# Compression blocks laid out by pairs of neighbouring positions, with one weight transfer per unit

## The chip, the cores and the metric

One core of a Trainium2 chip runs the whole two-layer decoder trunk as a single program. The metric is the device time in microseconds of one execution; the median of 3 runs before the change is 643.1 us (642.93 to 644.03).

## The reference, cut to what matters

The trunk has a gated convolution layer, a SwiGLU layer, sparse attention with three branches and a second SwiGLU layer, for 256 tokens of 1024 features, all in float32. The change touches the compressed branch of the attention alone:

```
L_CMP, D_CMP, G, DH = 32, 16, 4, 64        # block length, step, groups, head size
def compress(kv_raw, pe, w1, w2):           # once for keys, once for values
    idx = arange(15)[:, None] * D_CMP + arange(L_CMP)[None, :]
    blocks = kv_raw[:, idx] + pe            # 15 blocks of 32 tokens, overlapping by 16
    blocks = blocks -> [15, G, 32 * 64]
    return silu(blocks @ w1) @ w2           # w1: 2048 x 256, w2: 256 x 64
```

Block n covers the tokens 16n to 16n+31, so each token stands in two blocks. The position embedding pe is the same for every block; its product with w1 is added to each block's result as a share.

## The kernel before, in words

Every float32 operand of a matrix product is held as a high part (rounded by a copy on ScalarE) and a low part (the rest, a subtraction on VectorE), and a product is two or three matmuls. A weight comes in units of up to 128 x 1024. `split_weights` (L302) issues the unit's transfer on SP's queue into one of four raw buffers, copies the high part on ScalarE (L322), and subtracts on VectorE or GpSimd (L326). `Stream.ahead` issues a unit, `take` hands it to the matmuls.

The stage between the first SwiGLU layer and the attention follows a list of items, CFG["plan"]. K, Q, V and Y are projection units, Y being w1 (two sets st, four units q each); CR scales a projection into cf (L762); CB builds the blocks (`cmp_blocks`, L764); Y multiplies (`cmp_piece`, L780); J, M, t, ck, cv finish the compression. Between the marks `|4` and `|5` of the plan no engine's order is written out: a planner with a cost model of its own orders the instructions of all engines, SP's queue with them. From `|5` on TensorE follows the plan, and the planner orders the other engines. CB0 and CB1 and the first Y units stand between the two marks.

cf holds the compressed keys or values with features on the partitions: two groups above each other on 64 partitions each, two pairs of groups side by side, 256 tokens. `cmp_blocks` makes of it the stationary operand xc, 128 partitions x (high and low) x 4 groups x 256 columns: the upper 64 partitions hold token t, the lower 64 token t+16. That takes four ScalarE copies (L777) and four VectorE subtractions (L778) for each st, each of 64 partitions x 480 elements. The last 16 columns hold pe (L772, through `split`, L418 and L421), which thereby becomes a sixteenth block.

`cmp_piece` multiplies: for each of 16 positions lp in the half block, the stationary operand is the 128 columns (high and low, group, block n) that lie 16 elements apart, and the moving one 256 columns of w1's high part (L788), then of its low part (L789): 64 matmuls for both st. Since w1 lies in memory with rows of two neighbouring positions above each other, and the operand has positions lp and lp+16 above each other, each unit comes in two transfers of 64 rows (L314 to L316).

pe is loaded early, in the convolution stage, into a constant tile peT by two small transfers (L632). In that stage TensorE's and GpSimd's orders are as written (L597).

Of the kernel before, what the change touches and what calls it, by code (L numbers as in the profile page):

```python
# [10 lines left out]
AF = mybir.ActivationFunctionType  # L11
ALU = mybir.AluOpType
# [4 lines left out]
P = 128  # L17
D = 1024
S = 256
# [4 lines left out]
G = 4  # L24
DH = 64
NCMP = 16
# [201 lines left out]
def trunk(ctx: ExitStack, tc: tile.TileContext, a):  # L228
    nc = tc.nc
# [11 lines left out]
    def in_order(*engines):  # L241

        if "order" in phase:
            phase.pop("order").close()
        if engines:
            phase["order"] = ctx.enter_context(ExitStack())
            phase["order"].enter_context(tc.manual_schedule(engines=set(engines)))
# [14 lines left out]
    def bank(name, kind="short", hold=False):  # L262

        b = min((b for b in ring[kind] if b not in held.values()), key=used.get)
        touch(b)
        if hold:
            held[name] = b
        return psum.tile([P, 512], F32, tag=f"b{b}", name=name)
# [7 lines left out]
    def f(ap):  # L276
        return ap.bitcast(F32)

    def four(name):
        return [bank(f"{name}_{b}", "long") for b in range(4)]  # L280
# [4 lines left out]
    def pair(name, shape, rows=P):  # L285

        return act.tile([rows, 2, *shape], F32R, tag="pair", name=name, bufs=3)

    def one(name, cols=S, rows=P, dt=F32):

        return tmp.tile([P, S + 2], dt, tag="one", name=name, bufs=8)[:rows, :cols]
# [10 lines left out]
    def split_weights(src, name, cols, ring, pool):  # L302
        if (name[0], ring) in spare:
            w, hi, lo = spare.pop((name[0], ring))
        else:
            if phase["name"] == "attention" or name[0] == "O" or name[:2] == "kv":
                w = wp.tile([P, 1024], F32, tag="raw", name=f"w_{name}", bufs=4)
            else:
                w = phase["pool"].tile([P, 1024], F32, tag="raw", name=f"w_{name}", bufs=12)
            hi, lo = (wp.tile([P, 1024], F32R, tag=ring + hl, name=f"{hl}_{name}", bufs=3) for hl in "hl")  # L310
            if name[0] == "O":
                spare[name[0], ring] = [x[:, cols:] for x in (w, hi, lo)]
            w, hi, lo = (x[:, :cols] for x in (w, hi, lo))
        if isinstance(src, list):  # L314
            for r, part in enumerate(src):
                nc.sync.dma_start(out=w[r * DH:(r + 1) * DH], in_=part)  # L316
        else:
            nc.sync.dma_start(out=w, in_=src)
        if pool in ("hi", "all"):
            nc.gpsimd.tensor_copy(hi, w)  # L320
        else:
            nc.scalar.activation(hi, w, AF.Copy)  # L322
        cut = {False: 0, True: cols, "both": cols // 2, "hi": 0, "all": cols}[pool]
        for eng, c0, c1 in ((nc.gpsimd, 0, cut), (nc.vector, cut, cols)):
            if c0 < c1:
                eng.tensor_tensor(out=lo[:, c0:c1], in0=w[:, c0:c1], in1=f(hi[:, c0:c1]), op=ALU.subtract)  # L326
        return hi, lo
# [33 lines left out]
    takes = {}  # L361
# [4 lines left out]
            takes[f"Q{s}{'ab'[p]}"] = a["w_q"][s, p], 1024  # L366
    for q in range(4):
        for st in range(2):

            w1 = a["w1"][st, q % 2 * DH:(q % 2 + 1) * DH]  # L370
            takes[f"Y{st}{q}"] = [w1[:, x * 1024:(x + 1) * 1024] for x in (q // 2, 2 + q // 2)], 1024
        takes[f"V{q}"] = a["w_v"][q], 1024
    takes["GP"] = a["w_g"], KC * 48

# [41 lines left out]
    def split(hi, lo, src, key="ad"):  # L416
        if key[0] == "a":
            nc.scalar.activation(hi, src, AF.Copy)  # L418
        else:
            nc.gpsimd.tensor_copy(hi, src)  # L420
        (nc.gpsimd if key[1] == "p" else nc.vector).tensor_tensor(out=lo, in0=src, in1=f(hi), op=ALU.subtract)  # L421
# [8 lines left out]
    peT = const.tile([P, 2, NCMP], F32, name="peT")  # L430
# [79 lines left out]
    def residual_step(accs, u, x, first, chunks=range(KC)):  # L510
        for o in chunks:
            mm3(acc_at(accs, o), columns(u, o), x, first and o % 2 == 0, False)
# [36 lines left out]
    def stream_in(c, n=1):  # L549
        nc.sync.dma_start(out=h[:, c:c + n], in_=xT[:, c:c + n])  # L550
        for i in range(c, c + n):
            n0.high(i)
            n0.low(i)
# [10 lines left out]
    def conv_proj(pcv, pb, u, k0, n=2):  # L564
        for k in range(k0, k0 + n):
            for i, o in enumerate((pcv[:, :S], pcv[:, S:], pb[:, :S])):
                col = (3 * (k - k0) + i) * P
                mm3(o, sl(u, ALL, slice(col, col + P)), sl(x0, ALL, k), k == 0 and i != 1, k == KC - 1)
# [20 lines left out]
    def hidden(m, name):  # L589
        mh, ml = (phase["pool"].tile([P, S], F32R, tag=f"m{hl}", name=f"{name}_{hl}", bufs=4) for hl in "hl")  # L590
        split(mh, ml, m)
        return mh, ml

    ps, us, accs = {}, {}, None
    for j in range(KC):
        if j == 1:
            in_order(*ORD[9])  # L597

        ps[j] = [bank(f"{n}{j}", "long" if j == 2 else "short") for n in ("pcv", "pb")]
        for p in range(4):  # L600
            if j == 0 and p == 0:
                for k in range(2):
                    conv_proj(*ps[j], wa.take(), k, 1)
                    wa.ahead()
                    if k == 0:
                        stream_in(6, 2)
            else:
                conv_proj(*ps[j], wa.take(), 2 * p)
                wa.ahead()
            if j == 0:  # L610
                n0.square(2 * p)
                n0.square(2 * p + 1)
            if j == 1 and p == 1:
                n0.rstd()
            if j == 1 and p == 2:
                n0.spread()
                nc.vector.tensor_tensor(out=r2, in0=n0.bc, in1=n0.bc, op=ALU.mult)
                us[0] = conv_rest(0, *ps[0])
            if p == 2 and j:
                wr.ahead(min(j, 3))  # L620
            if p == 1 and j >= 2:
                gated.append(hidden(us[j - 1], f"m{j - 1}"))
            if p == 3 and j == 1:
                gated.append(hidden(us[0], "m0"))
        if j:
            us[j] = conv_rest(j, *ps[j])
        if j == 1:
            for t, n in ((dist, "dist"), (cdist, "cdist"), (rowvis, "rowvis")):
                nc.sync.dma_start(out=t, in_=a[n])
            for half in range(2):  # L630
                rows = slice(half * DH, half * DH + DH)
                nc.sync.dma_start(out=peT[rows], in_=a["peT"][rows, :, half * NCMP:(half + 1) * NCMP])  # L632
        if j == 2:
            accs = four("acc0")
        if j >= 2:
            residual_step(accs, wr.take(), gated[j - 2], j == 2)
# [121 lines left out]
    cf, xc, ys_, w2s, py = {}, {}, {}, {}, {}  # L758
# [5 lines left out]
    def cmp_blocks(st):  # L764

        if not xc:
            blocks = pair("xc", [2, G, S])
            xc.update({i: blocks[:, i] for i in range(2)})  # L770
        pe = peT[:, st].unsqueeze(1).to_broadcast([P, G, NCMP])
        split(xc[st][:, 0, :, S - 16:], xc[st][:, 1, :, S - 16:], pe)  # L772
        for gp in range(2):
            for half in range(2):
                src = cf[st][gp * DH:gp * DH + DH, :, 16 * half:S - 16 + 16 * half]
                dst = xc[st][half * DH:half * DH + DH, :, gp::2, :S - 16]
                nc.scalar.activation(dst[:, 0], src, AF.Copy)  # L777
                nc.vector.tensor_tensor(out=dst[:, 1], in0=src, in1=f(dst[:, 0]), op=ALU.subtract)  # L778

    def cmp_piece(st, q):  # L780
        if q == 0:
            py[st] = bank(f"py{st}", hold=True)
        wh, wl = wa.take()
        for i in range(4):
            lp = 8 * (q // 2) + 2 * i + q % 2
            first, last = q == 0 and i == 0, q == 3 and i == 3
            x = xc[st].rearrange("p hl g (n l) -> p l (hl g) n", l=16)[:, lp]
            nc.tensor.matmul(py[st][:, :256], x, wh[:, i * 256:(i + 1) * 256], start=first, stop=False)  # L788
            nc.tensor.matmul(py[st][:, :256], x, wl[:, i * 256:(i + 1) * 256], start=False, stop=last)  # L789

# [333 lines left out]
    for item in plan:  # L1124
        m = re.match(r"([A-Z|][A-Z]?|[a-z]+)(.*)", item)
# [40 lines left out]
    for t in range(2):  # L1166
        ms = EPS

        for c, part in ((0, slice(0, 512)), *((1, slice(x, x + n)) for n in (512 // (t + 1),)
# [5 lines left out]
            cols = slice(c * 512 + part.start, c * 512 + part.stop)  # L1175
# [3 lines left out]
            else:  # L1179
                nc.vector.tensor_tensor(out=hT[:, t, c * 512:(c + 1) * 512], in0=accs[2 * t + c],  # L1180
                                        in1=hT[:, t, c * 512:(c + 1) * 512], op=ALU.add)
# [6 lines left out]
            m = tmp.tile([P, 1], F32, tag="ms", name=f"fin_ms{t}{cols.start}", bufs=3)  # L1188
# [85 lines left out]
```

## Time and profile before

| | |
|---|---|
| median of 3 runs | 643.1 us (642.93 to 644.03) |
| profiled execution | 642.83 us, its span 641.0 us |
| granted TensorE clock, mean | 0.995 |
| TensorE busy | 619.5 us of the span, 97% |
| VectorE busy | 471.2 us, 74% |
| ScalarE busy | 377.4 us, 59% |
| GpSimd busy | 279.4 us, 44% |
| transfers | 109.53 MB, mean 171 GB/s |

The span runs from the first to the last instruction; what lies around it is 1.83 us. The convolution takes about the first 100 us, the first SwiGLU layer lasts to about 290 us, projections, compression and attention to about 440 us, and the second SwiGLU layer takes the rest. A busy engine is one with an instruction under way. TensorE's matmuls overlap in the pipeline, so the distance between starts, not the duration of one, is what a matmul costs.

### The profile page before, as it was taken

Reading aid. Unit: us, or ns where it says so; the run is one execution under the profiler, and the core shown is the slowest. Engines: PE = TensorE matmul, PEld = TensorE weight load, DVE = VectorE, ACT = ScalarE, POOL = GpSimd, SP = SyncE. Lnnn points to the kernel's source line nnn. Section 1 sums busy time; section 2 is a strip of 40 time slices with the busy share of each in tenths; the row PEclk is TensorE's granted clock in tenths of the full one; section 3 lists DMA queues with packets and bytes.
Section 4 is the critical chain, followed back from the end, with each engine's and each line's share of the span. In section 5 each row is a group of like instructions: output and inputs, shape, how many; then the busy total and the mean of one; then the engine's idle time right before and its main releaser. Section 6 shows DMA issues by size and latency. Waiting matters only on the chain.

```text
span 641.0 us, 11285 instructions
## 1 busy us (share of the span) xinstructions
PE 619.5 (97%) x4158; PEld 568.4 (89%) x4158; DVE 471.2 (74%) x783; ACT 377.4 (59%) x738; POOL 279.4 (44%) x258
## 2 busy tenths in 40 slices
PE   7999999999999999999999999997999999999995
PEld 6999999889999999999989998986888888888894
DVE  5789767866666666679996899787876666666664
ACT  7454447464455555547766988986565555555433
POOL 4054313854443334315100756567754433344423
PEclk9999999999999999999989999999999999999998
DMA  8996672646555554032978410009946655555001
GB/s 289 357 351 216 220 237 94 230 165 201 194 196 183 181 177 152 2 99 68 238 196 258 159 67 2 34 2 361 399 158 198 196 182 182 176 184 165 1 1 66
DMA packets 36360, 109.53 MB, mean 171 GB/s; under 512 B 5713, under 2 KB 8145, under 8 KB 36305
## 3 DMA queue, kind: packets, MB, share of 16 engines
q1 hardware_dynamic: 36160, 108.55, 51.2%
q8 instruction: 33, 0.54, 0.3%
q10 hardware_dynamic: 144, 0.26, 0.1%
q14 instruction: 23, 0.18, 0.1%
HBM read 107.22 MB, written 1.05 MB: 169 GB/s over the span
## 4 chain that ended last, share of the span: by engine, by line
PE 81%; DVE 10%; POOL 4%; issue 2%; DMA 1%; ACT 1%; SPq 0%; POOLq 0%; DVEq 0%; ACTq 0%
PE pgu L658 21%; PE pgu L660 11%; PE acc L397 4%; PE acc L398 4%; PE acc L396 4%; PE acc L726 3%; PE acc L725 3%; PE acc L724 3%; PE pcv L398 2%; DVE n L451 2%; PE pcv L397 2%; PE pcv L396 2%; PE po L1060 1%; POOL l_d L326 1%; PE pgu L398 1%
## 5 line engine op out<-in xcount | busy, mean ns | idle before, releaser
L658 PE MATMUL pgu<-n,h_gu 128*128 128x512 f32 x640 | 226.8, 397 | 2.9 <-DVE n L451 2.8
L660 PE MATMUL pgu<-n,l_gu 128*128 128x256 f32 x640 | 179.3, 281 | 1.1 <-DVE l_gu L326 1.1
L658 PEld LDWEIGHTS pgu<-n,h_gu 128*128 128x128 f32 x640 | 120.1, 188 | 31.0 <-DVE n L451 3.0
L326 DVE TENSOR_TENSOR l_gu<-w_gu,h_gu 128x1024 fp32r<-128x1024 f32 x88 | 117.1, 1332 | 26.6 <-ACT h_gu L322 26.1
L672 POOL TENSOR_TENSOR gu<-gu,n_rbc 128x512 f32<-128x512 f32 x40 | 54.8, 1374 | 166.1 <-DVE gu L667 150.0
L660 PEld LDWEIGHTS pgu<-n,l_gu 128*128 128x128 f32 x640 | 121.0, 189 | 2.3 <-DVE l_gu L326 1.4
L680 DVE TENSOR_TENSOR av<-sg,gu 128x256 f32<-128x256 f32 x44 | 74.4, 1692 | 65.7 <-ACT sg L678 65.5
L326 POOL TENSOR_TENSOR l_d<-w_d,h_d 128x1024 fp32r<-128x1024 f32 x40 | 98.0, 2452 | 4.9 <-ACT h_d L322 4.4
L322 ACT ACTIVATE h_gu<-w_gu 128x1024 fp32r<-128x1024 f32 x88 | 92.6, 1053 | 7.1 <-PE pb L397 3.5
L322 ACT ACTIVATE h_d<-w_d 128x1024 fp32r<-128x1024 f32 x44 | 46.8, 1063 | 27.1 <-PE acc L726 21.2
L418 ACT ACTIVATE a_h<-av 128x256 fp32r<-128x256 f32 x44 | 18.3, 416 | 72.8 <-DVE av L680 72.8
L678 ACT ACTIVATE sg<-gu 128x256 f32<-128x256 f32 x44 | 18.2, 416 | 58.9 <-POOL gu L672 54.2
L397 PE MATMUL acc<-a_l,h_d 128*128 128x256 f32 x176 | 49.5, 282 | 0.3 <-DVE a_l L421 0.3
L396 PE MATMUL acc<-a_h,h_d 128*128 128x256 f32 x176 | 49.3, 282 | 0.5 <-ACT a_h L418 0.5
L398 PE MATMUL acc<-a_h,l_d 128*128 128x256 f32 x176 | 49.3, 281 | 0.0
L326 DVE TENSOR_TENSOR l_in<-w_in,h_in 128x768 fp32r<-128x768 f32 (+1 forms) x33 | 38.8, 1187 | 11.4 <-ACT h_in L322 11.4
L322 ACT ACTIVATE h_in<-w_in 128x768 fp32r<-128x768 f32 (+1 forms) x33 | 27.1, 824 | 30.4 <-PE pb L397 21.8
L398 PE MATMUL pcv<-n,l_in 128*128 128x256 f32 x128 | 36.8, 288 | 1.8 <-DVE l_in L326 1.7
L396 PE MATMUL pcv<-n,h_in 128*128 128x256 f32 x128 | 36.8, 287 | 1.7 <-ACT h_in L322 1.7
L397 PE MATMUL pcv<-n,h_in 128*128 128x256 f32 x128 | 36.4, 284 | 0.0
L665 ACT ACTIVATE gu<-pgu 128x256 f32<-128x256 f32 x80 | 29.6, 370 | 10.9 <-PE pgu L660 10.9
L724 PE MATMUL acc<-h_d,a_h 128*128 128x512 f32 (+1 forms) x88 | 34.8, 395 | 0.0
(428 smaller groups left out, 1666.2 us busy)
## 6 DMA issues: line engine op xcount, KB each, us to landing
w_gu<-in_w_gu SPq DMA_DIRECT2D x88, 512.0 KB, 4.2
w_d<-in_w_down SPq DMA_DIRECT2D x44, 512.0 KB, 3.4
w_in<-in_w_in SPq DMA_DIRECT2D x31, 384.0 KB, 6.4
w_wo<-in_w_out SPq DMA_DIRECT2D x8, 512.0 KB, 6.3
w_kvY<-in_w SPq DMA_DIRECT2D x16, 256.0 KB, 5.1
w_kvV<-in_w_v SPq DMA_DIRECT2D x4, 512.0 KB, 5.9
h<-in_xT SPq DMA_DIRECT2D x3, 256.0 KB, 6.2
out<-y SPq DMA_DIRECT2D x3, 256.0 KB, 2.3
```

The costliest lines, as they stand in the source:

```text
L322: nc.scalar.activation(hi, w, AF.Copy)
L326: eng.tensor_tensor(out=lo[:, c0:c1], in0=w[:, c0:c1], in1=f(hi[:, c0:c1]), op=ALU.subtract)
L396: nc.tensor.matmul(out, wh, xh, start=start, stop=False, skip_group_check=True)
L397: nc.tensor.matmul(out, wh, xl, start=False, stop=False, skip_group_check=True)
L398: nc.tensor.matmul(out, wl, xh, start=False, stop=stop, skip_group_check=True)
L658: nc.tensor.matmul(ps[j][c], uh[:, cols], x[:, :, k], start=k == 0, stop=False, skip_group_check=True)
L660: nc.tensor.matmul(ps[j][c][:, :S], ul[:, cols], x[:, 0, k], start=False, stop=k == KC - 1, skip_group_check=True)
L665: nc.scalar.activation(gus[j][:, c], ps[j][c][:, S:], AF.Copy)
L672: nc.gpsimd.tensor_tensor(out=gu, in0=gu, in1=norm.bc.unsqueeze(1).to_broadcast([P, 2, S]), op=ALU.mult)
L680: nc.vector.tensor_tensor(out=av, in0=sg, in1=gu[:, 1], op=ALU.mult)
L724: nc.tensor.matmul(out, xh, wh, start=start, stop=False, skip_group_check=True)
L725: nc.tensor.matmul(out, xh, wl, start=False, stop=False, skip_group_check=True)
```

## The change

The operand xc is laid out by pairs. The upper 64 partitions hold the even tokens, the lower 64 the odd ones, so that a column j is the pair of tokens 2j and 2j+1. It is stored twice, "late" = 0 and late = 1, the second copy shifted by 16 tokens (8 pairs). Each copy has its last 8 columns for pe. The tile has as many bytes as before. A st now takes eight copies and eight subtractions of 64 partitions x 240 elements, which read cf at every second token. The columns of a stationary operand lie 8 elements apart instead of 16; the number of matmuls is the same. Rows of w1 are used as they lie, so a unit is one transfer of 128 rows; the list form of `split_weights` goes. pe is loaded by one transfer into a temporary tile of the tag "one" (8 buffers), and two GpSimd copies sort its even and odd positions into peT.

```diff
-        if isinstance(src, list):
-            for r, part in enumerate(src):
-                nc.sync.dma_start(out=w[r * DH:(r + 1) * DH], in_=part)
-        else:
-            nc.sync.dma_start(out=w, in_=src)
+        nc.sync.dma_start(out=w, in_=src)
...
-            w1 = a["w1"][st, q % 2 * DH:(q % 2 + 1) * DH]
-            takes[f"Y{st}{q}"] = [w1[:, x * 1024:(x + 1) * 1024] for x in (q // 2, 2 + q // 2)], 1024
+            takes[f"Y{st}{q}"] = a["w1"][st, :, q * 1024:(q + 1) * 1024], 1024
...
+            pe = one("pe", cols=4 * NCMP).rearrange("p (st m two) -> p st m two", st=2, two=2)
+            nc.sync.dma_start(out=pe.rearrange("p st m two -> p st (m two)"), in_=a["peT"])
             for half in range(2):
                 rows = slice(half * DH, half * DH + DH)
-                nc.sync.dma_start(out=peT[rows], in_=a["peT"][rows, :, half * NCMP:(half + 1) * NCMP])
+                nc.gpsimd.tensor_copy(peT[rows], pe[rows, :, :, half])
...
-            blocks = pair("xc", [2, G, S])
-            xc.update({i: blocks[:, i] for i in range(2)})
-        pe = peT[:, st].unsqueeze(1).to_broadcast([P, G, NCMP])
-        split(xc[st][:, 0, :, S - 16:], xc[st][:, 1, :, S - 16:], pe)
+            blocks = pair("xc", [2, 2, G, P])
+            xc.update({i: blocks[:, i].rearrange("p late hl g j -> p hl late g j") for i in range(2)})
+        pe = peT[:, st].rearrange("p (late m) -> p late m", late=2).unsqueeze(2).to_broadcast([P, 2, G, 8])
+        split(xc[st][:, 0, :, :, P - 8:], xc[st][:, 1, :, :, P - 8:], pe)
         for gp in range(2):
-            for half in range(2):
-                src = cf[st][gp * DH:gp * DH + DH, :, 16 * half:S - 16 + 16 * half]
-                dst = xc[st][half * DH:half * DH + DH, :, gp::2, :S - 16]
-                nc.scalar.activation(dst[:, 0], src, AF.Copy)
-                nc.vector.tensor_tensor(out=dst[:, 1], in0=src, in1=f(dst[:, 0]), op=ALU.subtract)
+            for odd in range(2):
+                dst = xc[st][odd * DH:odd * DH + DH, :, :, gp::2, :P - 8]
+                for late in range(2):
+                    src = cf[st][gp * DH:gp * DH + DH].rearrange("p c (j two) -> p c j two", two=2)[
+                        :, :, 8 * late:P - 8 + 8 * late, odd]
+                    hi, lo = dst[:, 0, late], dst[:, 1, late]
+                    nc.scalar.activation(hi, src, AF.Copy)
+                    nc.vector.tensor_tensor(out=lo, in0=src, in1=f(hi), op=ALU.subtract)
...
-            lp = 8 * (q // 2) + 2 * i + q % 2
+            late, m = divmod(4 * q + i, 8)
             first, last = q == 0 and i == 0, q == 3 and i == 3
-            x = xc[st].rearrange("p hl g (n l) -> p l (hl g) n", l=16)[:, lp]
+            x = xc[st][:, :, late].rearrange("p hl g (n m) -> p m hl g n", m=8)[:, m]
+            x = x.rearrange("p hl g n -> p (hl g) n")
```

## Rows read from the trace of the kernel before

**Rows 1.** The page's busy times of the engines over the whole span.

```profile
PE 619.5 (97%) x4158; PEld 568.4 (89%) x4158; DVE 471.2 (74%) x783; ACT 377.4 (59%) x738; POOL 279.4 (44%) x258
```

**Rows 2.** Windows: length, busy time of each engine, granted clock, DMA share, GB/s.

```profile
0.00:40.00 40.00, 34.75 (x255) 33.12 (x256) 27.29 (x42) 23.46 (x41) 13.17 (x20) 1.00 0.94 339
...
302.00:322.00 20.00, 19.90 (x166) 19.90 (x167) 18.50 (x29) 13.44 (x20) 3.34 (x2) 1.00 0.80 211
322.00:331.00 9.00, 7.79 (x38) 7.11 (x36) 8.87 (x12) 5.22 (x8) 0.00 (x0) 0.96 0.80 207
331.00:354.00 23.00, 23.00 (x134) 21.68 (x134) 16.97 (x27) 15.43 (x26) 1.57 (x3) 0.94 0.86 256
```

**Rows 3.** The timeline of TensorE around the first products of the blocks: start, duration.

```profile
322.21 0.28 PE L398 MATMUL pkv<-n,l_kvK4b 128*128 128x256 f32 x1
322.33 0.39 PE L788 MATMUL py<-h_kvY,xc 128*128 128x256 f32 x1
322.56 0.38 PE L789 MATMUL py<-l_kvY,xc 128*128 128x256 f32 x1
...
326.88 0.27 PE L788 MATMUL py<-h_kvY,xc 128*128 128x256 f32 x1
328.37 0.49 PE L789 MATMUL py<-l_kvY,xc 128*128 128x256 f32 x1 [1.22 <-DVE l_kvY L326]
```

**Rows 4.** The timeline of VectorE in the same stretch.

```profile
315.13 5.44 DVE L778 TENSOR_TENSOR xc<-cf,xc 64x480 fp32r<-64x480 f32 x8
320.59 1.23 DVE L326 TENSOR_TENSOR l_kvY<-w_kvY,h_kvY 128x1024 fp32r<-128x1024 f32 x1
...
322.34 1.21 DVE L326 TENSOR_TENSOR l_kvV<-w_kvV,h_kvV 128x1024 fp32r<-128x1024 f32 x1
...
325.66 1.40 DVE L421 TENSOR_TENSOR q<-qf,q 64x512 fp32r<-64x512 f32 x2
327.09 2.36 DVE L326 TENSOR_TENSOR l_kvY<-w_kvY,h_kvY 128x1024 fp32r<-128x1024 f32 x2
...
331.62 1.23 DVE L326 TENSOR_TENSOR l_kvY<-w_kvY,h_kvY 128x1024 fp32r<-128x1024 f32 x1 [0.25 <-ACT h_kvY L322]
```

**Rows 5.** The tile xc's instructions: count, ns shortest/median/longest, first and last start.

```profile
L789 PEld LDWEIGHTS py<-l_kvY,xc x32: 292/317/326, 322.4 to 343.0; 128*128 128x128 f32 x32
L777 ACT ACTIVATE xc<-cf x8: 589/604/607, 313.7 to 318.1; 64x480 fp32r<-64x480 f32 x8
L778 DVE TENSOR_TENSOR xc<-cf,xc x8: 642/654/658, 315.1 to 319.9; 64x480 fp32r<-64x480 f32 x8
L418 ACT ACTIVATE xc<-peT x2: 238/240/242, 300.8 to 300.9; 128x64 fp32r<-128x64 f32 x2
L421 DVE TENSOR_TENSOR xc<-peT,xc x2: 222/222/223, 305.0 to 305.2; 128x64 fp32r<-128x64 f32 x2
```

**Rows 6.** The timeline of ScalarE in the same stretch.

```profile
313.74 5.00 ACT L777 ACTIVATE xc<-cf 64x480 fp32r<-64x480 f32 x8
...
324.14 1.06 ACT L322 ACTIVATE h_kvY<-w_kvY 128x1024 fp32r<-128x1024 f32 x1 [0.40 <-ACT q L418]
326.44 1.06 ACT L322 ACTIVATE h_kvY<-w_kvY 128x1024 fp32r<-128x1024 f32 x1 [1.24 <-DMA w_kvY<-in_w]
```

**Rows 7.** Windows of 4 us: the fullest DMA, and TensorE at the lower clock.

```profile
310.00:314.00 4.00, 4.00 (x36) 4.00 (x35) 3.30 (x6) 2.28 (x3) 0.00 (x0) 1.00 1.03 238
...
330.00:334.00 4.00, 4.00 (x19) 4.00 (x20) 3.57 (x5) 3.11 (x5) 0.53 (x1) 0.57 0.90 222
```

**Rows 8.** The transfers of the Y units: their issue on SP, and issue to landing.

```profile
L316 SPq DMA_DIRECT2D w_kvY<-in_w x16: 465/576/590, 306.6 to 331.4; - x16
...
DMA to landing us min/median/max: 3.4/5.1/6.4
```

**Rows 9.** The timeline of GpSimd in the convolution stage.

```profile
39.35 2.39 POOL L326 TENSOR_TENSOR l_wo<-w_wo,h_wo 128x1024 fp32r<-128x1024 f32 x1
...
43.95 0.74 POOL L586 TENSOR_TENSOR u<-u,b 128x256 f32<-128x256 f32 x1 [2.17 <-DVE u L584]
```

## The prediction

> **What bounds the kernel now.** First the busy times: TensorE has work for 97% of the span [rows 1], so a change elsewhere counts only where it ends a wait of TensorE or makes one, and a change on TensorE counts by the distance between starts. Then the windows, for the stage that the diff touches. From 302 to 322 us TensorE is full (19.90 of 20.00) and VectorE nearly so (18.50). From 322 to 331 TensorE has 7.79 of 9.00 and VectorE 8.87: for these 9 us VectorE is the bound. From 331 to 354 TensorE is full again (23.00) and VectorE has some 6 us free (16.97) [rows 2]. Then the timelines of that stretch. TensorE's one wait there stands at 328.37: 1.22 us for a low part of a Y unit [rows 3]. VectorE shows why that came late: it makes the blocks from 315.13 to 320.57, then low parts and other subtractions without a pause, splits q from 325.66, and comes to the missing low part at 327.09; its first pause after the blocks is at 331.62 [rows 4]. ScalarE had begun that unit's high part at 324.14, and it takes 1.06 us [rows 6], so neither ScalarE nor a transfer was late: VectorE was.
>
> A second bound hides in TensorE's busy time. A matmul of 256 columns against an ordinary weight starts 0.12 us after the one before (322.21 to 322.33), but one against xc 0.23 us (322.33 to 322.56) [rows 3]. Its weight load lasts 317 ns [rows 5]. [...] So the load of xc's columns, 64 bytes apart, sets the pace, not the product.
>
> **The change part by part.** *Blocks on VectorE.* Eight subtractions of 480 elements (654 ns) become sixteen of 240. Two rows fix the line: 64 elements cost 222 ns, 480 cost 654 ns [rows 5], so 1.04 ns an element and 155 ns apiece; 240 elements make 405 ns. The eight stand 5.44 us end to end, 0.68 each [rows 4], or 0.03 more than one lasts. Sixteen at 0.435 are 6.96 us: 1.52 us more. The reads now step over every second element, and no row shows that for VectorE. Bounds: no extra if the step is free, and 16 x 240 x 1.04 ns = 4.0 us if each element costs double, as the column loads of rows 3 do. I take none: 8 bytes is much nearer to the contiguous reads of rows 5 than to the 64 of the column loads.
>
> *Blocks on ScalarE.* By the same two sizes (240 and 604 ns, [rows 5]) 240 elements make 394 ns; eight in 5.00 us [rows 6] become sixteen at 0.415, 6.64 us: 1.64 us more. This runs beside VectorE's and a little ahead of it, so it is not added to it.
>
> *Where this lands.* VectorE has no pause from 315.13 to 331.62 [rows 4], so nothing covers its 1.52 us. With its order as it is, the low part of the V unit (begun at 322.34) and that of the Y unit at 327.09 come 1.5 us later, and TensorE's wait of 1.22 us grows to 2.7, or splits into two with that sum. After 331.62 VectorE has slack, but TensorE has none, so a delay of TensorE there is not made up. This term is +1.52. Its bounds: the planner sets VectorE's order anew. If it puts the Y unit's low part before the split of q (1.40 us, [rows 4]), TensorE's wait is mostly gone, about -1.2 to 0; if it lets another low part slip as that one has, another 1.2 to 2.
>
> *The columns' step, 64 to 32 bytes.* 64 matmuls at 0.23 instead of 0.12 us cost 64 x 0.11 = 7.0 us. The trace has no load at 32 bytes. Bounds: no gain (as at 64 bytes) or -7.0 (as contiguous); a loss is left out, since a smaller step is nearer to the contiguous one. I take no gain, because 32 bytes still separate every two columns by eight elements, as far from contiguous as the double price is likely to reach. [...]
>
> *The Y units' transfers.* Sixteen issues of 576 ns on SP and 5.1 us to landing [rows 8] become eight. While Y units load, the DMA engines are full (share 1.03) and move only 238 GB/s [rows 7]; at the kernel's start, with transfers of 128 rows, 339 at a share of 0.94 [rows 2]. So I expect them to land one or two microseconds sooner and SP to be freer by 8 x 0.58 = 4.6 us in all. On TensorE's path this is worth nothing by itself, because the late low part waited for VectorE. The ScalarE wait that does show a transfer (1.24 us at 326.44) is for the following unit, which had no wait on TensorE [rows 3, 6]. Bounds: 0 to -1.2, the whole wait, if the earlier data changes the planner's order. I take 0. [...]
>
> *pe.* One transfer instead of two on SP, and two GpSimd copies of 64 partitions x 32 elements. They stand in GpSimd's written order behind the product of the second unit, so the low part of a w_out unit (39.35, 2.39 us) and what follows is queued behind them; GpSimd waits 2.17 us before the next product at 43.95 [rows 9]. That pause hides two copies, which at the price of the low part's 1024 columns are under 0.3 us. If the transfer's temporary tile were not free in time, SP would hold up w_in behind it, in a stage where the DMA share is 0.94 [rows 2]: some microseconds. I take 0, as most tiles of that tag hold squares that are used up by then.
>
> **Sum.** +1.52 + 0 + 0 + 0, against the profiled execution: 642.83 + 1.52 = 644.35. The median before, 643.1, is 0.27 above that execution, so I predict 644.6, 0.23% above the median.
>
> **The rivals.** *A. Forecast.* VectorE's 1.5 us stands in front of the Y units' low parts; own range 643.2 to 645.9, chance 0.42.
>
> *B. The planner's order swallows it.* Fewer, quicker transfers bring the high parts forward and the low part goes ahead of q's split. For it: nothing of this stage's order is written out. Against it: the late unit's high part was there in time already [rows 6]. 642.83 + 1.52 - 1.2 to -2.5 gives 641.9 to 643.2; chance 0.20.
>
> *C. The other side: the 32-byte step is cheap.* Then the loads cost what contiguous ones do. About 10 of the 64 matmuls start before 328.4, where VectorE rules, so 54 x 0.11 = 5.9 us could go; from 331 on the wait for low parts and transfers takes the place (DMA share 0.86, [rows 2]), and I count 4. 642.83 + 1.52 - 4 = 640.3, and 638.4 with all of 5.9. It decides once more than 1.5 us are saved, at a start distance below about 0.20 us. For it: the load is a whole bound by itself. Against it: two columns are still eight elements apart, and no row has a load at that step. [...] Chance 0.18.
>
> *D. Slower still.* Either VectorE and ScalarE pay double for reading every second token (+1.52 + 4.0: 648.4), or a second low part is put off (+1.5 + 2: 646.3). Chance 0.16.
>
> *E. pe's transfer stalls SP early.* 645 to 648; chance 0.04.
>
> **How the numbers follow.** Changes under 0.2% (1.3 us: 641.8 to 644.4) can't be told from none. Faster: C 0.16 and B 0.08, 0.24. Same: A 0.18, B 0.12, C 0.02, D and E 0.02, 0.34. Slower: A 0.24, D and E 0.18, 0.42. The range 640.0 to 647.4 leaves out about half of C and the dearer half of D and E.
>
> **What would show it.** Right: sixteen subtractions of about 405 ns in 7 us; starts against xc still 0.22 us apart; Y transfers of 512 KB that land in less than 5.1 us; TensorE's wait for l_kvY near 2.7 us in all. Wrong: starts 0.12 us apart (C); subtractions near 650 ns (D); no wait for l_kvY before TensorE's Y matmuls (B); SP waiting at the new transfer of pe before 40 us (E).

## The result, and the profile after

The changed kernel takes 649.6 us (median of 4 runs, 649.13 to 649.78) against 643.0 (642.55 to 644.03) before: a ratio of 1.0099, 95% interval 1.0085 to 1.0114. It is slower by 6.6 us. That is above the forecast of 644.6, and above the range's upper end of 647.4. The profiled execution took 649.67 us with a span of 647.9, 6.9 more than before.

Four marks cut the span into stages: the end of the convolution (the first addition of its output to h), the first matmul against the blocks xc, the first transposition of their product (pyT), and the end of the attention (the first addition of its output to h).

| stage ends at (us) | before | after | longer by |
|---|---|---|---|
| convolution | 102.65 | 106.43 | 3.8 |
| first product of xc | 322.33 | 326.34 | 0.2 |
| first pyT | 343.46 | 349.75 | 2.3 |
| attention | 439.01 | 445.87 | 0.6 |

So more than half of the loss is already there at the end of the convolution, in a stage where the diff touches only the loading of pe. The page's busy times say that TensorE is busy for 4.5 us more than before [rows 1], VectorE as long as before.

```profile
PE 624.0 (96%) x4158; PEld 572.2 (88%) x4158; DVE 471.0 (73%) x791; ACT 379.2 (59%) x746; POOL 279.9 (43%) x260
```

*The convolution stage.* First, windows of two stretches, before and then after (columns as in rows 2):

```profile
40.00:50.00 10.00, 10.00 (x86) 10.00 (x85) 8.48 (x8) 5.07 (x8) 6.35 (x5) 1.00 0.67 244
50.00:60.00 10.00, 9.80 (x83) 9.60 (x82) 8.66 (x10) 4.87 (x7) 4.84 (x5) 1.00 0.73 221
```

```profile
40.00:50.00 10.00, 7.63 (x62) 7.42 (x62) 5.77 (x4) 4.00 (x6) 8.29 (x8) 1.00 0.49 168
50.00:60.00 10.00, 9.55 (x67) 9.55 (x68) 6.77 (x10) 3.57 (x5) 2.65 (x2) 0.83 0.63 212
```

After, TensorE starts 24 matmuls fewer in the first of them (62 instead of 86). In the second it is busy, but starts 16 fewer, at a mean granted clock of 0.83: behind the pause, from 52 to 55 us, it is 0.50, and matmuls start 0.21 us apart instead of 0.12. Three timelines of the changed kernel tell why: SP's issue of pe, then GpSimd [rows 9], then VectorE.

```profile
31.52 0.33 SPq L625 DMA_DIRECT2D pe<-in_peT  x1
```

```profile
37.68 0.72 POOL L580 TENSOR_TENSOR u<-u,b 128x256 f32<-128x256 f32 x1 [2.92 <-DVE u L578]
39.80 0.47 POOL L628 COPY peT<-pe 64x32 f32<-64x32 f32 x2 [1.40 <-ACT h_wo L318]
40.35 2.40 POOL L322 TENSOR_TENSOR l_wo<-w_wo,h_wo 128x1024 fp32r<-128x1024 f32 x1
42.69 0.11 POOL L571 MEMSET z<- 128x2 f32 x1
```

```profile
42.83 1.01 DVE L578 SCALAR_TENSOR_TENSOR u<-z,gains,u 128x256 f32<-128x256 f32 x2 [2.94 <-POOL z L571]
45.20 2.17 DVE L415 TENSOR_TENSOR m_l<-u,m_h 128x256 fp32r<-128x256 f32 x1 [1.37 <-ACT m_h L412]
47.30 4.84 DVE L322 TENSOR_TENSOR l_in<-w_in,h_in 128x768 fp32r<-128x768 f32 x3
...
318.95 6.43 DVE L777 TENSOR_TENSOR xc<-cf,xc 64x240 fp32r<-64x240 f32 x15
...
326.67 0.41 DVE L777 TENSOR_TENSOR xc<-cf,xc 64x240 fp32r<-64x240 f32 x1
```

pe is issued at 31.52 us; the two small transfers of before went out at 17.03. It takes 8.2 us to land, so until 39.7, and GpSimd's copies start at 39.80 (the row names a high part of ScalarE, but the copies don't read that). In GpSimd's written order the low part of w_out and the clearing of z stand behind the copies. From the product u to that clearing 5.0 us pass (37.68 to 42.69), where it was 3.0 (38.67 to 41.68). VectorE waits 2.94 us for z. Then it makes m_l, and only after it, from 47.30 to 52.14, three low parts of w_in that TensorE needs. Before, the first of them came ahead of m_l, at 44.27. The rows of before for this, two of GpSimd and one of VectorE:

```profile
38.67 0.72 POOL L586 TENSOR_TENSOR u<-u,b 128x256 f32<-128x256 f32 x1 [2.92 <-DVE u L584]
41.68 0.10 POOL L577 MEMSET z<- 128x2 f32 x1
44.27 1.24 DVE L326 TENSOR_TENSOR l_in<-w_in,h_in 128x768 fp32r<-128x768 f32 x1 [0.47 <-ACT h_in L322]
```

TensorE waits 2.82 us in the changed kernel, as the first row of its timeline says (the others are for the compression):

```profile
50.45 0.39 PE L392 MATMUL pcv<-n,l_in 128*128 128x256 f32 x1 [2.82 <-DVE l_in L322]
...
326.34 0.40 PE L788 MATMUL py<-h_kvY,xc 128*128 128x256 f32 x1
326.58 0.40 PE L789 MATMUL py<-l_kvY,xc 128*128 128x256 f32 x1
...
333.75 0.51 PE L789 MATMUL py<-l_kvY,xc 128*128 128x256 f32 x1 [2.06 <-DVE l_kvY L322]
```

*The compression.* Sixteen subtractions now take 6.43 + 0.41 us, where eight took 5.44 [rows 4]. TensorE's wait for the low part of a Y unit grows from 1.22 us [rows 3] to 2.06. Starts against xc stand 0.241 us apart (326.34 to 328.03 for seven, at a clock of 1.00). Before they stood 0.223 apart (322.33 to 323.89, also at 1.00). By tiles, of xc (count, ns shortest/median/longest [rows 5]) and of the raw Y units [rows 8]:

```profile
L789 PEld LDWEIGHTS py<-l_kvY,xc x32: 312/337/341, 326.4 to 349.3; 128*128 128x128 f32 x32
...
L776 ACT ACTIVATE xc<-cf x16: 397/411/421, 317.7 to 324.5; 64x240 fp32r<-64x240 f32 x16
L777 DVE TENSOR_TENSOR xc<-cf,xc x16: 393/402/408, 319.0 to 326.7; 64x240 fp32r<-64x240 f32 x16
```

```profile
L314 SPq DMA_DIRECT2D w_kvY<-in_w x8: 328/328/346, 310.5 to 334.9; - x8
...
DMA to landing us min/median/max: 3.7/5.2/6.1
```

### The profile page after: what moved, and what is told of

The parts are those of the page before. It is cut to its first block, busy times and chain, and to the rows that moved or that the text cites. A ratio compares the mean times of both kernels' runs of the same rounds, so it can differ in the third digit from the quotient of the medians.

```text
span 647.9 us, 11283 instructions
## 1 busy us (share of the span) xinstructions
PE 624.0 (96%) x4158; PEld 572.2 (88%) x4158; DVE 471.0 (73%) x791; ACT 379.2 (59%) x746; POOL 279.9 (43%) x260
## 4 chain that ended last, share of the span: by engine, by line
PE 77%; DVE 12%; POOL 4%; issue 3%; ACT 2%; DMA 2%; SPq 0%; POOLq 0%; DVEq 0%; ACTq 0%
PE pgu L654 21%; PE pgu L656 11%; PE acc L391 4%; PE acc L392 4%; PE acc L390 4%; PE acc L721 3%; PE acc L722 3%; PE acc L720 3%; DVE n L445 2%; PE pcv L392 2%; PE pcv L391 2%; PE pcv L390 2%; PE po L1060 1%; POOL l_d L322 1%; DVE p L982 1%
## 5 line engine op out<-in xcount | busy, mean ns | idle before, releaser
L654 PEld LDWEIGHTS pgu<-n,h_gu 128*128 128x128 f32 x640 | 120.7, 189 | 31.5 <-DVE n L445 3.1
L318 ACT ACTIVATE h_gu<-w_gu 128x1024 fp32r<-128x1024 f32 x88 | 92.7, 1054 | 7.0 <-PE pb L391 3.5
L322 DVE TENSOR_TENSOR l_in<-w_in,h_in 128x768 fp32r<-128x768 f32 (+1 forms) x33 | 35.3, 1078 | 10.1 <-ACT h_in L318 8.8
```

The lines of the kernel that those rows point to most:

```text
L654: nc.tensor.matmul(ps[j][c], uh[:, cols], x[:, :, k], start=k == 0, stop=False, skip_group_check=True)
```

## The experiments

Ratios are to the kernel before, run on the same chip beside them, with their 95% interval. The rows were measured on several chips, so two of them are compared by their ratios.

| kernel | median us | ratio |
|---|---|---|
| changed kernel | 649.6 | 1.0099 [1.0085, 1.0114] |
| pe_only | 647.35 | 1.0064 [1.0046, 1.0082] |
| pe_direct | 645.88 | 1.0041 [1.0026, 1.0056] |
| pe_own_tile | 645.12 | 1.0032 [1.0018, 1.0046] |
| one_transfer | 642.14 | 0.9983 [0.9972, 0.9994] |
| halved | 644.56 | 1.0032 [1.0020, 1.0045] |
| inner_r | 643.01 | 1.0005 [0.9995, 1.0015] |
| inner_w | 643.94 | 1.0019 [1.0010, 1.0028] |
| pair_r | 642.47 | 0.9993 [0.9983, 1.0002] |
| pair_w | 642.32 | 0.9994 [0.9984, 1.0004] |
| steps | 643.72, one run | |

**Is it pe, and what of it?** Theory: the temporary tile's buffer comes free late, so the transfer goes out late and GpSimd's copies wait for it. Rivals: the copies themselves cost it, or the loss before 322 us has nothing to do with pe.

*pe_only* is the kernel before with nothing changed but pe:

```diff
+            pe0 = one("pe", cols=4 * NCMP)
+            pe = pe0.rearrange("p (st two m) -> p st two m", st=2, two=2)
+            nc.sync.dma_start(out=pe0.rearrange("p (st x) -> p st x", st=2), in_=a["peT"])
             for half in range(2):
...
-                nc.sync.dma_start(out=peT[rows], in_=a["peT"][rows, :, half * NCMP:(half + 1) * NCMP])
+                nc.gpsimd.tensor_copy(peT[rows], pe[rows, :, :, half])
```

> The kernel before, with one part of the change alone: pe comes by one transfer into a temporary tile and two GpSimd copies bring it into peT. Blocks, columns and w1's transfers are as before. Theory P (pe's path costs most of the loss: its transfer waits for a free temporary tile, lands about 39 us, GpSimd's written order waits for it, and the planner has put the low parts of w_in behind it): about 4 us slower than before, 646.5 to 648, with TensorE waiting some 2.8 us near 50 us. Theory Y (the loss is made in the compression): 643, no change.

*pe_direct* is the changed kernel with pe sorted beforehand and loaded by two transfers, as before:

```diff
-            pe = one("pe", cols=4 * NCMP).rearrange("p (st m two) -> p st m two", st=2, two=2)
-            nc.sync.dma_start(out=pe.rearrange("p st m two -> p st (m two)"), in_=a["peT"])
             for half in range(2):
...
-                nc.gpsimd.tensor_copy(peT[rows], pe[rows, :, :, half])
+                nc.sync.dma_start(out=peT[rows], in_=a["peT"][rows, :, half * NCMP:(half + 1) * NCMP])
```

> The changed kernel with pe's path alone undone: two small transfers straight into peT, as before (pe lies sorted by parity in memory). Theory P: 645 to 646, which is 3.5 to 4.5 us faster than the changed kernel and about 2 to 3 slower than before, the rest being the blocks' extra instructions and slower column loads. Theory Y: 649, as the changed kernel.

*pe_own_tile* is the changed kernel with one transfer and both copies kept, but a buffer of its own:

```diff
-            pe = one("pe", cols=4 * NCMP).rearrange("p (st m two) -> p st m two", st=2, two=2)
+            pe = const.tile([P, 4 * NCMP], F32, name="pe").rearrange("p (st m two) -> p st m two", st=2, two=2)
```

> The changed kernel with pe's temporary tile replaced by one of its own, so that its transfer need not wait for a buffer; the two GpSimd copies stay where they are. Theory P1 (the late buffer makes the loss): the transfer goes out near 16 us and the time is that of the kernel with pe loaded directly, 645 to 646. Theory P2 (the two copies in GpSimd's order make it, or their 0.5 us): about 649, as the changed kernel.

pe_only alone loses 4.3 us (647.35 against 643.05; by the interval 3.0 to 5.3). Without the temporary tile the changed kernel gets 3.7 us back (pe_direct), with a tile of its own 4.5 (pe_own_tile; 4.3 by the ratios). So it is pe, and of pe the buffer: in pe_own_tile the transfer goes out at 16.28, and both copies still stand in GpSimd's order. Its timelines of SP, GpSimd and VectorE:

```profile
16.28 0.33 SPq L625 DMA_DIRECT2D pe<-in_peT  x1
```

```profile
37.37 0.72 POOL L580 TENSOR_TENSOR u<-u,b 128x256 f32<-128x256 f32 x1 [2.92 <-DVE u L578]
38.04 1.13 POOL L628 COPY peT<-pe 64x32 f32<-64x32 f32 x2
...
41.65 0.10 POOL L571 MEMSET z<- 128x2 f32 x1
```

```profile
41.78 1.01 DVE L578 SCALAR_TENSOR_TENSOR u<-z,gains,u 128x256 f32<-128x256 f32 x2 [2.33 <-POOL z L571]
42.98 1.45 DVE L322 TENSOR_TENSOR l_in<-w_in,h_in 128x768 fp32r<-128x768 f32 x1 [0.19 <-ACT h_in L318]
44.36 2.63 DVE L415 TENSOR_TENSOR m_l<-u,m_h 128x256 fp32r<-128x256 f32 x1
```

The wait for the landing, which the theory had at its centre, is only part of it. The same two timelines of pe_only:

```profile
40.07 0.72 POOL L586 TENSOR_TENSOR u<-u,b 128x256 f32<-128x256 f32 x1 [2.92 <-DVE u L584]
40.74 1.29 POOL L635 COPY peT<-pe 64x32 f32<-64x32 f32 x2
...
44.45 0.10 POOL L577 MEMSET z<- 128x2 f32 x1
```

```profile
44.59 1.00 DVE L584 SCALAR_TENSOR_TENSOR u<-z,gains,u 128x256 f32<-128x256 f32 x2 [2.29 <-POOL z L577]
46.96 2.16 DVE L421 TENSOR_TENSOR m_l<-u,m_h 128x256 fp32r<-128x256 f32 x1 [1.37 <-ACT m_h L418]
49.04 4.86 DVE L326 TENSOR_TENSOR l_in<-w_in,h_in 128x768 fp32r<-128x768 f32 x3
```

Its transfer, issued at 32.3, has landed when GpSimd gets to the copies, and z is cleared 4.4 us after the product, as in pe_own_tile (4.3). VectorE waits as long for z (2.29 and 2.33 us). What differs is the order behind it: the planner, with the transfer late in SP's order, has put a high and a low part of w_in behind m_h and m_l. In this stage pe_only and the changed kernel have the same order on all engines. From that product to the end of the convolution pe_own_tile takes 63.8 us (before: 64.0), pe_only 66.6, the changed kernel 68.8. So in these single profiles the order costs 2.6 to 2.9 us, and the changed kernel's longer wait of GpSimd, with the lower clock after it, another 2.1.

One thing in pe_only's profile is not pe's. It comes to that product at 40.07 us, the kernel before at 38.67, and most of this lateness is there by 16 us, before the two orders first differ (SP's, at 17 us): from 10 to 20 us its granted clock is 0.66, where it was 1.00. The changed kernel, by the same order, comes there at 37.68. So pe_only's first product of xc, at 326.63, stands near the changed kernel's 326.34 by luck. In the changed kernel's profile, with its earlier arrival, GpSimd gets to the copies before pe has landed; in pe_only's it does not.

**One transfer for a unit.** *one_transfer* is the kernel before with w1's rows arranged beforehand, so that a unit is one transfer of 128 rows. Blocks and pe are those of before.

```diff
-            w1 = a["w1"][st, q % 2 * DH:(q % 2 + 1) * DH]
-            takes[f"Y{st}{q}"] = [w1[:, x * 1024:(x + 1) * 1024] for x in (q // 2, 2 + q // 2)], 1024
+            takes[f"Y{st}{q}"] = a["w1"][st, :, q * 1024:(q + 1) * 1024], 1024
```

> The kernel before, with w1 lying in memory so that each Y unit comes in one transfer of 128 rows; blocks and pe as before, and the order of all engines but SP the same. Theory H (the quicker transfer is hidden, since VectorE was late and not the data): 643, within 0.2%. Theory B (the earlier data shortens TensorE's wait of 1.22 us): 641.5 to 642.3.

A small gain, 0.9 us (0.9983 [0.9972, 0.9994]), with the order of all engines but SP unchanged. It meets the figures of both theories, so it does not decide between them. The transfers land after 4.7 us instead of 5.1, and TensorE's wait for the low part is 1.02 instead of 1.22 us. That is 0.2 of the 0.9; where the rest comes from stays open, since the profiled execution (643.33 us) is no faster than that of before.

**The blocks in twice as many pieces.** *halved* is one_transfer with each copy and subtraction cut in two of 240 elements, contiguous and at the old column step, so that only the number of instructions changes, and with it the planner's order.

```diff
-                src = cf[st][gp * DH:gp * DH + DH, :, 16 * half:S - 16 + 16 * half]
-                dst = xc[st][half * DH:half * DH + DH, :, gp::2, :S - 16]
+                for t0 in (0, 120):
+                    src = cf[st][gp * DH:gp * DH + DH, :, 16 * half + t0:16 * half + t0 + 120]
+                    dst = xc[st][half * DH:half * DH + DH, :, gp::2, t0:t0 + 120]
...
```

> The one-transfer kernel with each of the eight copies and eight subtractions cut in two of 240 elements, contiguous reads, columns 64 bytes apart as before. Theory V (VectorE's extra time stands in front of the low parts): 16 x 0.43 = 6.9 us instead of 5.4, TensorE's wait grows from 1.0 to about 2.2 us, 643.2 to 643.8, or 1.2 to 1.6 us over the one-transfer kernel; with the dearer column load (64 x 0.018 = 1.2 us) that makes up the 2.2 us that the changed blocks cost up to the first transposes. Rival V0 (the planner hides it): 642, as the one-transfer kernel.

It loses 2.4 us against one_transfer (644.56 and 642.14; by the ratios to before 0.0049, or 3.1 us), more than the 1.2 to 1.6 expected. By xc's instructions, and by TensorE's longest wait from 320 to 350 us:

```profile
L773 DVE TENSOR_TENSOR xc<-cf,xc x16: 393/402/406, 315.8 to 323.5; 64x240 fp32r<-64x240 f32 x16
```

```profile
PE py L784 <- DVE l_kvY L322: 2.1, 1, 2.1
```

402 ns for contiguous pieces is exactly what the changed kernel's pieces take: reading every second token costs VectorE nothing. From the first product to pyT it takes 22.70 us (one_transfer 20.90): the wait for a low part is 1.1 us longer, and one of 0.5 for the low part of a V unit is new. From pyT to the attention's end it takes 0.9 more, and there two waits are new, one for pt (0.6 us) and one for w2s (0.4). pe_direct shows the same two, with 0.6 and 0.4 as well.

What is left of the changed kernel's compression is the column load. pe_direct needs 23.31 us from the first product to pyT, 2.4 more than one_transfer: 1.1 of longer wait, and 64 x 0.0185 = 1.2 us for starts 0.241 instead of 0.223 us apart.

**What the columns' step costs.** *steps* is one_transfer whose stationary operand is read at steps of 1 to 16 elements, one step for each unit. It multiplies other columns than the blocks', so only its times mean something.

```diff
-            x = xc[st].rearrange("p hl g (n l) -> p l (hl g) n", l=16)[:, lp]
+            by = ((1, 2, 4, 8), (16, 12, 6, 3))[st][q]
+            x = xc[st].rearrange("p hl g t -> p (hl g t)")[:, i:i + 127 * by + 1:by]
```

> The one-transfer kernel, whose stationary operands are read at other steps, so that they hold other columns than the blocks' (the values of the compression are changed): Y00 reads xc at 1 element, Y01 at 2, Y02 at 4, Y03 at 8, Y10 at 16, Y11 at 12, Y12 at 6, Y13 at 3. The orders of all engines are the same. Theory L (a load costs double from some step on, whatever the step): starts 0.12 us apart at 1, 2 and perhaps 3 elements, about 0.22 from 4 or 6 on, and 8 elements no dearer than 16. Theory S (the price depends on the step itself, and 32 bytes are worse than 64): 0.24 at 8 elements and 0.22 at 16, as the changed kernel and the kernel before show, with other prices between.

TensorE's timeline has, two by two, starts at steps of 1, 2, 4, 16 and 3 elements:

```profile
322.10 0.28 PE L783 MATMUL py<-h_kvY,xc 128*128 128x256 f32 x1
322.22 0.28 PE L784 MATMUL py<-l_kvY,xc 128*128 128x256 f32 x1
...
328.31 0.28 PE L783 MATMUL py<-h_kvY,xc 128*128 128x256 f32 x1
328.43 0.28 PE L784 MATMUL py<-l_kvY,xc 128*128 128x256 f32 x1
...
329.56 0.39 PE L784 MATMUL py<-l_kvY,xc 128*128 128x256 f32 x1
329.79 0.40 PE L783 MATMUL py<-h_kvY,xc 128*128 128x256 f32 x1
...
332.18 0.39 PE L783 MATMUL py<-h_kvY,xc 128*128 128x256 f32 x1
332.40 0.38 PE L784 MATMUL py<-l_kvY,xc 128*128 128x256 f32 x1
...
342.51 0.33 PE L783 MATMUL py<-h_kvY,xc 128*128 128x256 f32 x1
342.68 0.34 PE L784 MATMUL py<-l_kvY,xc 128*128 128x256 f32 x1
```

| step, elements (bytes) | 1 (4) | 2 (8) | 3 (12) | 4 (16) | 6 (24) | 8 (32) | 16 (64) |
|---|---|---|---|---|---|---|---|
| us between starts | 0.12 | 0.12 | 0.175 | 0.233 | 0.228 | 0.241 | 0.222 |

All of them are at a granted clock of 1.00, except the 8 elements (0.85 in that stretch; the changed kernel has the same 0.241 at 1.00). The 12 elements (48 bytes), 0.267 us, fell into a stretch at 0.50, the lower level, and are left out. At 32 and 64 bytes that level hardly changed the distance (0.240 us in the changed kernel from 335.12 to 337.28, 0.224 before from 330.54 to 331.66, both at 0.50), so 48 bytes may be dearer than either; no run shows them at 1.00. So in these runs the price is single at 4 and 8 bytes, half way between at 12, and about double at 16, 24, 32 and 64. That is theory S: the price depends on the step, and 32 bytes are dearer than 64 (0.241 and 0.222 us). The prediction's rival C, for whom 32 bytes had to be cheap, falls. Why it rises between 8 and 16 bytes, and what spreads it from 0.222 to 0.241 us above, no run shows.

**Can the operand be laid out for the load?** Four kernels on the base of one_transfer lay xc out so that the columns lie closer. *inner_r* puts them side by side, and the copies and subtractions write contiguously and read at every 16th element; *inner_w* has the same layout, read contiguously and written at a distance.

```diff
-                src = cf[st][gp * DH:gp * DH + DH, :, 16 * half:S - 16 + 16 * half]
+                src = cf[st][gp * DH:gp * DH + DH, :, 16 * half:S - 16 + 16 * half].rearrange("p c (n l) -> p c l n", l=16)
...
-            x = xc[st].rearrange("p hl g (n l) -> p l (hl g) n", l=16)[:, lp]
+            x = xc[st][:, :, lp].rearrange("p hl g n -> p (hl g n)")
```

> The one-transfer kernel with xc stored so that the 128 columns of a stationary operand lie next to each other: four copies and four subtractions per set as before, which now read cf 16 elements apart and write contiguous runs of 15. Theory L or S alike: the matmuls start 0.12 us apart, 64 x 0.10 = 6.5 us less, of which the wait for low parts keeps some: 637 to 639.5. Rival R (reads 64 bytes apart double the eight copies and the eight subtractions, 5 us more on VectorE in front of the low parts): 641 to 644, no gain.

> As inner_r, but the copies and subtractions read cf contiguously and write xc 128 elements apart. Theory W0 (a scattered write costs nothing more): subtractions of 0.65 us and 637 to 639.5. Rival W1 (it doubles them): subtractions above 1 us and 641 to 644.

The matmuls start 0.12 us apart in both, and neither is faster than before, as the rivals R and W1 had it. Of xc's instructions in inner_r:

```profile
L772 ACT ACTIVATE xc<-cf x8: 1041/1054/1074, 313.0 to 320.5; 64x480 fp32r<-64x480 f32 x8
L773 DVE TENSOR_TENSOR xc<-cf,xc x8: 993/998/1011, 314.4 to 321.6; 64x480 fp32r<-64x480 f32 x8
```

The distance has moved to ScalarE (604 to 1054 ns) and VectorE (654 to 998; with distant writes 1096). Eight subtractions are 2.8 us longer, on the engine that is the bound there.

*pair_r* and *pair_w* keep pairs of neighbouring positions together, so that the columns lie 8 bytes apart and the copies and subtractions touch pairs. pe's columns are then written last, and the order of the groups changes with it.

```diff
+                "p (lq hl s n lk) -> p hl lq s n lk", lq=8, hl=2, s=G, lk=2) for i in range(2)})
...
-            x = xc[st][:, :, lp].rearrange("p hl g n -> p (hl g n)")
+            x = xc[st][:, :, lp // 2, :, :, lp % 2].rearrange("p hl s n -> p (hl s n)")
```

> The kernel with one host-arranged transfer per w1 unit, and with a third layout of the blocks: positions in pairs, so that the columns of the stationary operand lie 2 elements (8 bytes) apart, where the run with mixed steps showed starts 0.12 us apart. ScalarE and VectorE write runs of 64 contiguous elements and read pairs of neighbours, 64 bytes from pair to pair (1.0 us per block instruction when single elements lay 64 bytes apart, 0.60 and 0.65 when contiguous). Theory 'half the rows, half the surcharge': about 0.82 us each, 8 x 0.17 = 1.4 us on VectorE, against 64 x 0.10 = 6.4 us of column loads less: 638 to 641. Rival 'strided anyway': 1.0 us each and TensorE waits for VectorE as in the run with fully contiguous columns: 642.5 to 643.5. Rival 'the low parts are the bound': starts 0.12 us apart, instructions near 0.65 us, and the time still within 1 us of one_transfer's 642, because TensorE waits for low parts instead.

> As the run before it, but ScalarE and VectorE read contiguously and write pairs of neighbours. Theory 'half the surcharge': about 0.85 us each, 638 to 641. Rival 'strided anyway': near 1.1 us each, about 643.5.

Neither half the surcharge nor all of it: there is none. By the tiles of pair_w:

```profile
L786 PEld LDWEIGHTS py<-l_kvY,xc x32: 193/195/201, 325.2 to 340.6; 128*128 128x128 f32 x32
L772 ACT ACTIVATE xc<-cf x8: 648/667/669, 313.1 to 318.0; 64x512 fp32r<-64x512 f32 x4, 64x496 fp32r<-64x496 f32 x4
L773 DVE TENSOR_TENSOR xc<-cf,xc x8: 673/676/685, 314.7 to 319.7; 64x512 fp32r<-64x512 f32 x4, 64x496 fp32r<-64x496 f32 x4
```

512 elements take 676 ns, no more than contiguous ones would at 1.04 ns each and 155. Load and blocks are both cheap now, and the time is still that of one_transfer (642.32 and 642.14; by the ratios 0.9994 and 0.9983). The 64 loads are cheaper by 64 x 0.10 = 6.4 us. The first product comes 2.4 us later (325.19, one_transfer 322.75), since pe's columns are written behind the blocks here, but twelve other matmuls stand before it for that, so this is no loss by itself. TensorE's longest waits from 300 to 442 us are new but for the first, which was 1.0:

```profile
PE py L786 <- DVE l_kvY L322: 1.8, 1, 1.8
PE py L785 <- ACT h_kvY L318: 1.5, 2, 1.1
PE pk L391 <- DVE hk L415: 1.1, 1, 1.1
```

Its pyT comes 2.8 us earlier than in one_transfer (340.88 against 343.65), and the attention ends 0.6 earlier (438.55, 439.19). From 320 us to pyT TensorE waits 3.9 us for high and low parts of the weights, where one_transfer waits 1.0: about half of the 6.4 us goes there, since ScalarE and VectorE make the parts hardly sooner (VectorE starts its two Y low parts in a row at 327.13 us, in one_transfer at 327.32). In the attention another 2.1 us are lost, of which the wait for hk is 1.1; the rest is not assigned. The third expectation, that the parts are the bound, came true in the time, and by the waits for about half of it. The lowest ratio is that of one_transfer, 0.17% under before; the intervals of pair_r and pair_w overlap with its own.

## Why the prediction was wrong

*The failed step is pe*: "I take 0, as most tiles of that tag hold squares that are used up by then." The price came from the two copies (under 0.3 us, hidden). In pe_own_tile they take 1.13 us, but no loss shows behind them: 63.8 us to the end of the convolution, 64.0 before. But with the temporary tile the transfer went out at 31.5 us instead of 16 to 17, and this costs 4.3 us (pe_only). "Most tiles" was no count: the eight buffers had to be set, from the code, against the tiles of that tag. The eight that the code asks for just before pe are not squares but v, z, b and u of the first two units (L568 to L575 of the changed kernel), and in the changed kernel the first of them is written at 24.93 us and none is read for the last time before 28.25. Which buffer pe got the trace does not say. Rival E had named the place of this loss, and a range (645 to 648) that pe_only's 647.35 meets, with a chance of 0.04. Its mechanism was half right. SP did not stand waiting at pe, since the planner put the issue where the buffer was free. The price came from what the planner then put behind other work on ScalarE and VectorE, and from GpSimd, whose written order waited for the landing.

*Blocks on VectorE, +1.52: right in kind, too small.* The duration is as worked out (402 ns against 405; 6.84 us against 6.96), and TensorE's wait grew to 2.06, where 2.7 was the forecast. That is 1.1 us more of waiting in halved too. But halved loses 2.4 to 3.1 us in all: the planner's new order brings two waits of 1.0 us in the attention, which the sum did not hold. The rival D's double price for every second token is not there.

*The columns' step, 0:* no gain, as forecast, but a loss that the bounds left out ("a loss is left out, since a smaller step is nearer to the contiguous one"). That the double price reaches to 32 bytes was the author's estimate, which no row of before shows. The runs show 0.241 us between starts there and 0.222 to 0.223 at 64 bytes: 32 bytes cost 1.2 us more than 64.

*The transfers, 0:* a gain of 0.9 us (one_transfer), inside the bounds. They landed in 5.2 us in the changed kernel, not "one or two microseconds sooner". The rate did rise as worked out from rows 7: from 310 to 314 us the changed kernel moves 305 GB/s at a share of 0.91, where it was 238 at 1.03.

The parts together: 4.3 (pe) + 2.4 to 3.1 (pieces) + 1.2 (column load) - 0.9 (transfers) = 7.0 to 7.7, and 6.6 were measured. The rest is within the intervals. Without pe's late buffer the changed kernel takes 645.1 to 645.9 us (pe_own_tile, pe_direct), inside rival A's own range of 643.2 to 645.9; that is partly luck, since the losses that the sum had at nothing (the columns' step, the waits in the attention) and the gain that it had at nothing (the transfers) cancel in part. *B*, the planner swallowing it, is refuted: its order added waits rather than took one away.

## What to carry to other kernels

A small load through a temporary tile cost here what its late buffer brought with it (4.3 us in pe_only), not what its copies took (1.13 us in pe_own_tile, and no loss behind them): find the tile that it must wait for, and follow who is put behind it. Where one load is the visible pace (here the columns of a stationary operand, 0.22 us a start instead of 0.12), first ask what comes next: taking away all of it gained nothing, since waits for the weights' parts took back about half, and the attention most of the rest. Where a planner orders the rest, an extra instruction can have a second price in a later stage (here two waits, 1.0 us together, in the attention), and the range should have room for it.

## What the runs showed of the hardware

- With a stationary operand of float32, matmuls of 256 columns started 0.12 us apart at 4 and 8 bytes from column to column, 0.175 at 12, and 0.22 to 0.24 at 16, 24, 32 and 64; 32 bytes were dearer than 64 (0.241 and 0.222). At 32 and 64 bytes the lower clock level (0.50) hardly changed the distance (0.240 and 0.224).
- ScalarE and VectorE pay for single elements read 64 bytes apart (604 to 1054 ns, 654 to 998; inner_r) and for single elements written 512 bytes apart (1074 and 1096; inner_w). VectorE does not pay for every second element (402 ns in the changed kernel and in halved), nor for pairs of neighbours, read 64 bytes from pair to pair (673 ns for 512, pair_r) or written 1024 bytes from pair to pair (676, pair_w).
- In the changed kernel the granted clock was 0.50 from 52 to 55 us, a little after TensorE's wait of 2.82 us, and matmuls started 0.21 us apart there instead of 0.12; from 50 to 60 us 16 fewer started than before. That the wait brought the lower clock is not shown: one of 2.2 us at the same place in pe_only left it at 1.00.
